# A two-layer hybrid encoder on one Trainium2 core: tile pools opened in another order, so that the matmul operands begin at multiples of 2 KB in each partition

## The chip, the cores and the metric

The kernel runs on one core of one Trainium2 chip. The metric is the device time of one execution in microseconds (us); lower is better. On-chip memory (SBUF) has 128 partitions, and every tile takes the same byte range in each of them. TensorE (PE in the profile) multiplies: a weight load (PEld) puts a stationary block of 128x128 into the array, and a matmul streams a moving block of 128 rows and up to 512 columns past it into PSUM. VectorE (DVE), ScalarE (ACT) and GpSimd (POOL) do elementwise work; SyncE (SP) issues most DMAs.

## The reference, cut to what matters

Two layers; each has a mixing half (windowed attention and an mLSTM side by side) and an MLP half. 256 tokens of width 2048, MLP width 8192, all in float32.

```
def hybrid_layer(x, w_in, ..., w_out, ..., w_up, w_down):
    h = rms_norm(x, g_pre_mix)
    proj = h @ w_in                                   # 2048 x 4624
    ...                                               # attention and mLSTM on slices of proj
    mix = jnp.concatenate([att, mem.astype(att.dtype)], axis=-1) @ w_out
    x = x + rms_norm(mix, g_post_mix)
    h = rms_norm(x, g_pre_mlp)
    u = jnp.square(jax.nn.relu(h @ w_up))             # 2048 x 8192
    x = x + rms_norm(u @ w_down, g_post_mlp)          # 8192 x 2048
    return x
```

## The kernel before, in words

All large products run as three float32r matmuls. Each operand is split into a high part (rounded to float32r) and a low part (what is left), and the product is high*high + high*low + low*high.

**Weights.** They arrive from `wall` in pieces of up to 1 MB, four pieces for one tile of 512 output columns. `load` puts a piece into `raw` by a DMA (SP queue), ACT copies it into `whi` (L186), DVE subtracts and writes `wlo` (L187). `raw` has two buffers (pool `wraw`), `whi` and `wlo` four each (pool `wsp`), so the pieces of the next tile are prepared under the matmuls of this one.

**Tokens.** The normed tokens, the attention output, the mLSTM output and the MLP's hidden values stand transposed, as high and low part, in tiles of 8x2x256 (`hT`, `attT`, `memT`, `h2T`, `uT`; pool `tpool`, 16 KB a buffer, four buffers). One block of 128 features holds 256 high values and behind them 256 low values, 1 KB each.

**Two kinds of matmul.** `mm_k` (L198 to L200) serves the "in", "out" and "down" stages and the first "up" tile: a token block of 128 columns is stationary, and a row of weights (512 columns, 2 KB in each partition; 272 and 256 in two of the "in" tiles) is moving. `mm_stationary` (L267 to L269) serves the other "up" tiles: a weight block of 128 columns is stationary and 256 token columns (1 KB) are moving. Every matmul loads its stationary block anew. The order on each engine is that of the program; waits are semaphores set from the data's dependences.

**Where tiles lie.** A pool takes its place in SBUF when it is opened, and tiles of one buffer follow each other in the order in which they are first asked for. Before the change `const` comes first (with `xs`, the 16 KB of residual stream, at its head), then `tpool`, `apool`, `gpool`, `wraw`, `wsp` and the small ones. 1152 bytes in front of all pools hold the DMA scratch and four constants. So the build gives these starts (bytes in each partition; a 512-wide row of weights that starts at remainder 1728 reaches over the next multiple of 2048, and so does the high half of a token block, which starts at 1664; its low half starts at 640 and does not):

| tile | start before | remainder by 2048 | start after | remainder by 2048 |
|---|---|---|---|---|
| tokens, buffers of `tpool` | 30336 + 16384 i | 1664 | 2048 + 16384 i | 0 |
| `whi` | 134848 + 8192 i | 1728 | 67584 + 8192 i | 0 |
| `wlo` | 167616 + 8192 i | 1728 | 100352 + 8192 i | 0 |
| `raw` | 118464 + 8192 i | 1728 | 133120 + 8192 i | 0 |
| `xs` | 1152 | 1152 | 149504 | 0 |
| `A_mix`, `A_out`, `A_mlp` | 95872 | 1664 | 177824 | 1696 |

In the 272-wide "in" tile the rows of a piece are 1088 bytes apart: before, its four rows start at remainders 1728, 768, 1856 and 896, so the second and fourth row start at a multiple of 128 and do not reach over a multiple of 2048, the first and third start 64 past a multiple of 128 and do. In the 256-wide tile they start at 1728 and 704 in turn, both 64 past a multiple of 128.

Of the kernel before, what the change touches and what calls it, by code (L numbers as in the profile page):

```python
# [10 lines left out]
F32 = mybir.dt.float32  # L11
# [6 lines left out]
P = 128  # L18
SEQ = 256
NT = SEQ // P  # L20
DM = 2048
DFF = 4 * DM
DEPTH = 2
KC = DM // P
# [7 lines left out]
NG = 36  # L32
# [53 lines left out]
@with_exitstack  # L86
def encoder_kernel(ctx, tc, x, wall, rope, conv_w, gate_bias, ml_g, sink, gpre, gpost, out):
    nc = tc.nc
    const = ctx.enter_context(tc.tile_pool(name="const", bufs=1))
    tpool = ctx.enter_context(tc.tile_pool(name="tpool", bufs=4))  # L90
    apool = ctx.enter_context(tc.tile_pool(name="apool", bufs=1))
    gpool = ctx.enter_context(tc.tile_pool(name="gpool", bufs=3))
    wraw = ctx.enter_context(tc.tile_pool(name="wraw", bufs=2))
    wsp = ctx.enter_context(tc.tile_pool(name="wsp", bufs=4))
    f2k = ctx.enter_context(tc.tile_pool(name="f2k", bufs=8))
    f1k = ctx.enter_context(tc.tile_pool(name="f1k", bufs=5))
    small = ctx.enter_context(tc.tile_pool(name="small", bufs=3))
# [2 lines left out]
    psax = ctx.enter_context(tc.tile_pool(name="psax", bufs=4, space=bass.MemoryType.PSUM))  # L100


    xs = const.tile([P, NT, DM], F32, name="xs")

    def load_x(t, n):
        sl = slice(n * 512, (n + 1) * 512)
        nc.sync.dma_start(xs[:, t, sl], x[t * P:(t + 1) * P, sl])

    load_x(0, 0)
    gcol = const.tile([P, 2 * DEPTH, KC], F32, name="gcol")  # L110
    nc.scalar.dma_start(gcol, gpre)
    ident = const.tile([P, P], F32, name="ident")
    make_identity(nc, ident)
# [13 lines left out]
    dmask = const.tile([P, 2, P], F32R, name="dmask")  # L127
    nc.scalar.activation(dmask, mbase, AF.Copy)
    cossin = const.tile([P, 2, NT, HD], F32, name="cossin")
    nhalf = const.tile([P, 4], F32, name="nhalf")  # L130
    nc.gpsimd.memset(nhalf, -0.5)
    gpad = const.tile([P, NT, 2, NG], F32, name="gpad")
    nc.gpsimd.memset(gpad, 0.0)
    ones_r = const.tile([NG, P], F32, name="ones_r")
    nc.gpsimd.memset(ones_r, 1.0)
# [818 lines left out]
```

## Time and profile before

| | |
|---|---|
| median of 3 runs | 2145.48 us (2144.82 to 2150.1) |
| the profiled execution: its own time | 2146.32 us |
| its span, first to last instruction | 2144.5 us |
| PE busy | 2101.9 us, 98% of the span |
| mean granted clock of TensorE | 0.995 |

The span leaves 1.8 us of the execution's time around it. PE is busy from end to end, and the matmuls overlap each other in the record: one shows 0.39 us while the next starts 0.23 us after it. What a matmul costs is therefore read from the distance of starts and not from its duration.

### The profile page before, as it was taken

To read this page: it belongs to the slowest core of one execution; us is meant where nothing else is said; L and a number is where in the kernel's file an instruction comes from. 1 tells how busy PE (TensorE), PEld (TensorE's weight loads), DVE (VectorE), ACT (ScalarE), POOL (GpSimd) and SP (SyncE) were. 2 spreads that over 40 slices of the span, in tenths; PEclk is the share of its full clock that TensorE was granted. 3 is DMA by queue.
4 is the path that set the end of the run, shared out by engine and by line. 5 is a ranking of instruction groups with operands and counts; after the bars stand their busy time and mean duration, and the time that the engine had idled before them with its cause. 6 is when DMAs were issued, how large, how long until landed. Compare 5 with 4: busy or idle time off the path is not lost.

```text
span 2144.5 us, 28977 instructions
## 1 busy us (share of the span) xinstructions
PE 2101.9 (98%) x12412; PEld 1847.2 (86%) x12412; DVE 1134.8 (53%) x1219; ACT 983.1 (46%) x1077; POOL 60.8 (3%) x68
## 2 busy tenths in 40 slices
PE   8999999999999999999999999999999999999998
PEld 6878887988998998898878788879889989989986
DVE  6656566544444444445566656464544454444454
ACT  5445545453443453345354555454444434533542
POOL 0000002000000000000020000030000000000000
PEclk9999999999999999999999999999999999999999
DMA  7434354555555455545444344535555555555553
GB/s 251 165 138 176 119 195 179 197 189 187 194 190 192 175 199 203 187 173 219 169 179 161 134 151 147 206 132 203 206 197 179 195 195 178 197 195 177 197 203 116
DMA packets 62209, 388.37 MB, mean 181 GB/s; under 512 B 9600, under 2 KB 10112, under 8 KB 17280
## 3 DMA queue, kind: packets, MB, share of 16 engines
q1 hardware_dynamic: 61936, 386.48, 51.2%
q8 instruction: 97, 1.59, 0.3%
q14 instruction: 32, 0.26, 0.0%
q10 hardware_dynamic: 144, 0.03, 0.0%
HBM read 384.39 MB, written 2.10 MB: 180 GB/s over the span
## 4 chain that ended last, share of the span: by engine, by line
PE 92%; DVE 2%; ACT 2%; DMA 2%; POOL 1%; issue 1%; SPq 0%; POOLq 0%; DVEq 0%; ACTq 0%
PE mm L200 20%; PE mm L198 19%; PE mm L199 19%; PE mms L267 10%; PE mms L269 10%; PE mms L268 10%; DMA raw<-wall 1%; DVE wlo L187 1%; PE pn L589 1%; PE sc L373 1%; PE po L412 1%; ACT whi L186 1%; DVE xs L787 1%; POOL h2T L320 1%; ACT uz L843 0%
## 5 line engine op out<-in xcount | busy, mean ns | idle before, releaser
L187 DVE TENSOR_TENSOR wlo<-raw,whi 128x2048 fp32r<-128x2048 f32 (+3 forms) x374 | 828.8, 2217 | 885.9 <-ACT whi L186 885.6
L186 ACT ACTIVATE whi<-raw 128x2048 fp32r<-128x2048 f32 (+3 forms) x374 | 693.2, 1854 | 926.9 <-PE mm L200 519.0
L267 PE MATMUL mms<-h2T,whi 128*128 128x256 f32 x1920 | 531.8, 277 | 7.2 <-ACT uz L843 6.6
L268 PE MATMUL mms<-h2T,whi 128*128 128x256 f32 x1920 | 529.9, 276 | 0.0
L269 PE MATMUL mms<-h2T,wlo 128*128 128x256 f32 x1920 | 527.2, 276 | 0.0
L198 PE MATMUL mm<-whi,uT 128*128 128x512 f32 x1024 | 403.7, 394 | 0.0
L200 PE MATMUL mm<-whi,uT 128*128 128x512 f32 x1024 | 401.2, 392 | 0.0
L199 PE MATMUL mm<-wlo,uT 128*128 128x512 f32 x1024 | 397.6, 388 | 0.0
L267 PEld LDWEIGHTS mms<-h2T,whi 128*128 128x128 f32 x1920 | 360.4, 188 | 12.0 <-ACT uz L843 10.6
L268 PEld LDWEIGHTS mms<-h2T,whi 128*128 128x128 f32 x1920 | 360.5, 188 | 0.4
L269 PEld LDWEIGHTS mms<-h2T,wlo 128*128 128x128 f32 x1920 | 358.9, 188 | 0.0
L198 PE MATMUL mm<-whi,hT 128*128 128x512 f32 (+2 forms) x640 | 242.2, 379 | 7.8 <-ACT hT L319 5.8
L200 PE MATMUL mm<-whi,hT 128*128 128x512 f32 (+2 forms) x640 | 242.0, 379 | 0.6 <-POOL hT L320 0.5
L199 PE MATMUL mm<-wlo,hT 128*128 128x512 f32 (+2 forms) x640 | 242.1, 378 | 0.2 <-DVE wlo L187 0.2
L200 PEld LDWEIGHTS mm<-whi,uT 128*128 128x128 f32 x1024 | 192.2, 188 | 44.6
L199 PEld LDWEIGHTS mm<-wlo,uT 128*128 128x128 f32 x1024 | 192.3, 188 | 42.5
L198 PEld LDWEIGHTS mm<-whi,uT 128*128 128x128 f32 x1024 | 192.7, 188 | 37.9
L198 PEld LDWEIGHTS mm<-whi,hT 128*128 128x128 f32 x640 | 121.5, 190 | 29.0 <-ACT hT L319 6.6
L200 PEld LDWEIGHTS mm<-whi,hT 128*128 128x128 f32 x640 | 121.4, 190 | 22.3 <-POOL hT L320 1.4
L199 PEld LDWEIGHTS mm<-wlo,hT 128*128 128x128 f32 x640 | 121.4, 190 | 20.8 <-DVE wlo L187 0.5
L864 DVE SCALAR_TENSOR_TENSOR A_mlp<-mm,s2q,A_mlp 128x512 f32<-128x512 f32 x48 | 34.0, 748 | 38.5 <-PE mm L200 38.5
L198 PE MATMUL mm<-whi,memT 128*128 128x512 f32 x128 | 50.6, 395 | 0.0
(221 smaller groups left out, 1464.4 us busy)
## 6 DMA issues: line engine op xcount, KB each, us to landing
raw<-wall SPq DMA_DIRECT2D x350, 1024.0 KB, 4.8
raw<-wall SPq DMA_DIRECT2D x8, 544.0 KB, 3.6
g<-gpost SPq DMA_DIRECT2D x16, 256.0 KB, 4.4
raw<-wall SPq DMA_DIRECT2D x8, 512.0 KB, 3.4
xs<-x_in SPq DMA_DIRECT2D x8, 256.0 KB, 6.3
raw<-wall SPq DMA_DIRECT2D x8, 256.0 KB, 6.2
y_out<-xs SPq DMA_DIRECT2D x8, 256.0 KB, 2.8
cossin<-rope SPq DMA_DIRECT2D x1, 256.0 KB, 7.2
```

Source lines behind the costliest of these rows:

```text
L186: nc.scalar.activation(hi[:, sl], raw[:, sl], AF.Copy)
L187: nc.vector.tensor_tensor(out=lo[:, sl], in0=raw[:, sl], in1=hi[:, sl].bitcast(F32), op=ALU.subtract)
L198: nc.tensor.matmul(dst, lhsT=xh, rhs=hi, start=(k == 0), stop=False)
L199: nc.tensor.matmul(dst, lhsT=xh, rhs=lo, start=False, stop=False)
L200: nc.tensor.matmul(dst, lhsT=xl, rhs=hi, start=False, stop=(k == KC - 1))
L267: nc.tensor.matmul(ps[:, i], lhsT=hi[:, k], rhs=Tk[:, 0], start=(k == 0), stop=False)
L268: nc.tensor.matmul(ps[:, i], lhsT=hi[:, k], rhs=Tk[:, 1], start=False, stop=False)
L269: nc.tensor.matmul(ps[:, i], lhsT=lo[:, k], rhs=Tk[:, 0], start=False, stop=(k == KC - 1))
L320: (eng or nc.vector).tensor_tensor(out=lo, in0=ps, in1=hi.bitcast(F32), op=ALU.subtract)
L373: nc.tensor.matmul(sc[:, j], lhsT=qT[:, q0 + j, t * P:(t + 1) * P], rhs=kT[:, g], start=(j == 0), stop=False)
L412: nc.tensor.matmul(po[:, j], lhsT=vA[:, kb, g * HD:(g + 1) * HD], rhs=pT[:, kb], start=(kb == 0), stop=(kb == 1))
L864: nc.vector.scalar_tensor_tensor(out=acc[:, t, sl], in0=ps, scalar=s2[t], in1=acc[:, t, sl], op0=ALU.mult, op1=ALU.add)
```

## The change

The pools are opened in another order. A new pool `edge` takes three small tiles that were in `const` (`gcol`, `nhalf`, `gpad`); `nhalf` grows from 4 to 16 columns, and with that `edge` fills exactly the 896 bytes from 1152 to 2048. Behind it stand `tpool`, `wsp` and `wraw`, whose buffers are multiples of 2 KB, and only then `const` and the others. The starts that this gives are in the table above. No buffer is added or dropped. The instructions of every engine stand in the same order with the same waits as before; the one that differs is the fill of `nhalf` (16 columns in place of 4).

```diff
@@ encoder_kernel
     nc = tc.nc
+    edge = ctx.enter_context(tc.tile_pool(name="edge", bufs=1))
+    tpool = ctx.enter_context(tc.tile_pool(name="tpool", bufs=4))
+    wsp = ctx.enter_context(tc.tile_pool(name="wsp", bufs=4))
+    wraw = ctx.enter_context(tc.tile_pool(name="wraw", bufs=2))
     const = ctx.enter_context(tc.tile_pool(name="const", bufs=1))
-    tpool = ctx.enter_context(tc.tile_pool(name="tpool", bufs=4))
     apool = ctx.enter_context(tc.tile_pool(name="apool", bufs=1))
     gpool = ctx.enter_context(tc.tile_pool(name="gpool", bufs=3))
-    wraw = ctx.enter_context(tc.tile_pool(name="wraw", bufs=2))
-    wsp = ctx.enter_context(tc.tile_pool(name="wsp", bufs=4))
...
+    gcol = edge.tile([P, 2 * DEPTH, KC], F32, name="gcol")
+    nhalf = edge.tile([P, 16], F32, name="nhalf")
+    gpad = edge.tile([P, NT, 2, NG], F32, name="gpad")
     xs = const.tile([P, NT, DM], F32, name="xs")
...
-    gcol = const.tile([P, 2 * DEPTH, KC], F32, name="gcol")
...
-    nhalf = const.tile([P, 4], F32, name="nhalf")
     nc.gpsimd.memset(nhalf, -0.5)
-    gpad = const.tile([P, NT, 2, NG], F32, name="gpad")
     nc.gpsimd.memset(gpad, 0.0)
```

## Rows read from the trace of the kernel before

**Rows 1.** The page, part 1: busy time, share of the span, instructions.
```profile
PE 2101.9 (98%) x12412; PEld 1847.2 (86%) x12412; DVE 1134.8 (53%) x1219; ACT 983.1 (46%) x1077; POOL 60.8 (3%) x68
```
**Rows 2.** The page, part 4: the chain that ended last, by engine.
```profile
PE 92%; DVE 2%; ACT 2%; DMA 2%; POOL 1%; issue 1%; SPq 0%; POOLq 0%; DVEq 0%; ACTq 0%
```
**Rows 3.** Groups by shape: busy us, mean ns of one, idle before.
```profile
L187 DVE TENSOR_TENSOR wlo<-raw,whi 128x2048 fp32r<-128x2048 f32 x350 | 803.3, 2296 | 859.7 <-ACT whi L186 859.5
L186 ACT ACTIVATE whi<-raw 128x2048 fp32r<-128x2048 f32 x350 | 671.1, 1917 | 892.6 <-PE mm L200 497.5 <-PE mms L268 207.9 <-DMA raw<-wall 170.1
L267 PE MATMUL mms<-h2T,whi 128*128 128x256 f32 x1920 | 531.8, 277 | 7.2 <-ACT uz L843 6.6 <-ACT whi L186 0.6
L198 PE MATMUL mm<-whi,uT 128*128 128x512 f32 x1024 | 403.7, 394 | 0.0
L198 PE MATMUL mm<-whi,hT 128*128 128x512 f32 x512 | 205.6, 402 | 7.8 <-ACT hT L319 5.8 <-ACT qkn L521 2.0
L198 PE MATMUL mm<-whi,memT 128*128 128x512 f32 x128 | 50.6, 395 | 0.0
L198 PE MATMUL mm<-whi,attT 128*128 128x512 f32 x128 | 50.5, 394 | 0.0
L198 PE MATMUL mm<-whi,h2T 128*128 128x512 f32 x64 | 25.9, 404 | 2.7 <-ACT h2T L319 2.7
```
**Rows 4.** Timeline of PE in a "down" tile: start us, us, what.
```profile
1000.17 0.39 PE L198 MATMUL mm<-whi,uT 128*128 128x512 f32 x1
1000.40 0.39 PE L199 MATMUL mm<-wlo,uT 128*128 128x512 f32 x1
1000.63 0.39 PE L200 MATMUL mm<-whi,uT 128*128 128x512 f32 x1
...
1002.23 0.39 PE L198 MATMUL mm<-whi,uT 128*128 128x512 f32 x1
```
**Rows 5.** Timeline of PE in an "up" tile.
```profile
400.02 0.28 PE L267 MATMUL mms<-h2T,whi 128*128 128x256 f32 x1
400.14 0.28 PE L268 MATMUL mms<-h2T,whi 128*128 128x256 f32 x1
400.25 0.28 PE L269 MATMUL mms<-h2T,wlo 128*128 128x256 f32 x1
400.36 0.28 PE L267 MATMUL mms<-h2T,whi 128*128 128x256 f32 x1
...
401.04 0.28 PE L267 MATMUL mms<-h2T,whi 128*128 128x256 f32 x1
```
**Rows 6.** Windows: length; busy us of PE, PEld, DVE, ACT, POOL; clock; DMA share; GB/s.
```profile
1000.00:1010.00 10.00, 10.00 (x45) 8.21 (x44) 7.20 (x6) 4.18 (x7) 0.00 (x0) 1.00 0.54 193
1315.00:1317.00 2.00, 2.00 (x19) 2.00 (x19) 2.00 (x7) 2.00 (x8) 0.00 (x0) 1.00 0.41 94
1325.60:1328.20 2.60, 2.60 (x26) 2.60 (x25) 1.24 (x6) 2.59 (x5) 0.00 (x0) 1.00 0.99 296
```
**Rows 7.** Timeline of PE in the 256-wide "in" tile of layer 2, two stretches.
```profile
1315.29 0.28 PE L198 MATMUL mm<-whi,hT 128*128 128x256 f32 x1
...
1316.70 0.28 PE L198 MATMUL mm<-whi,hT 128*128 128x256 f32 x1
...
1325.68 0.28 PE L198 MATMUL mm<-whi,hT 128*128 128x256 f32 x1
...
1328.06 0.28 PE L198 MATMUL mm<-whi,hT 128*128 128x256 f32 x1
```
**Rows 8.** Timeline of PE in the 272-wide "in" tile of layer 1.
```profile
99.88 0.28 PE L198 MATMUL mm<-whi,hT 128*128 128x272 f32 x1
...
100.63 0.29 PE L198 MATMUL mm<-whi,hT 128*128 128x272 f32 x1
...
101.38 0.28 PE L198 MATMUL mm<-whi,hT 128*128 128x272 f32 x1
...
102.12 0.28 PE L198 MATMUL mm<-whi,hT 128*128 128x272 f32 x1
...
102.88 0.39 PE L198 MATMUL mm<-whi,hT 128*128 128x512 f32 x1
```
**Rows 9.** The chain in the first 60 us: start us, us, what.
```profile
3.54 7.00 DMA xs<-x_in
...
24.63 8.55 DMA raw<-wall
```
**Rows 10.** Timeline of POOL at the start.
```profile
1.47 0.10 POOL L131 MEMSET nhalf<- 128x4 f32 x1
1.50 0.22 POOL L133 MEMSET gpad<- 128x144 f32 x1
```
**Rows 11.** Spans and mean granted clock.
```profile
core 0: 2144.5 us, clock 0.995
```

## The prediction

> **What bounds the kernel now.** I read the busy shares first, then the chain of work that ended last, then the groups by shape, and last the timeline of PE, row by row, in the places that the change could touch. PE is busy 98% of the span [rows 1] and makes up 92% of the chain; DVE, ACT and DMA have 2% each [rows 2]. The splitting of the weights, the largest work outside PE, waits and is not waited for: ACT stands idle before L186 because PE still holds the buffers, and DVE stands idle before L187 because ACT has not finished [rows 3]. So the time is the number of matmuls by the distance of their starts, and an edit that only moves tiles counts if it changes that distance.
>
> The distance has two values. In a "down" tile nine 512-wide matmuls lie between 1000.17 and 1002.23 us [rows 4]: 2.06/9 = 0.2289 us each. In an "up" tile nine 256-wide ones lie between 400.02 and 401.04 [rows 5]: 0.1133 us. The clock granted in the first place is 1.00, the level of 2.4 GHz [rows 6], where one column a cycle would be 0.2133 and 0.1067. So 15.6 ns of each 512-wide matmul and 6.7 ns of each 256-wide one are something else, and the question of this change is whether they hang on the operands' addresses. Counts: with three lines each, the 512-wide matmuls are 3 x (1024 + 512 + 128 + 128 + 64) = 5568, the 256-wide "up" ones 3 x 1920 = 5760 [rows 3]. That is 5568 x 0.2289 + 5760 x 0.1133 = 1274.5 + 652.6 = 1927 us of the span.
>
> **The change part by part.** Its parts are four: where the moving and stationary operands start, where the elementwise engines read and write, where DMAs land, and a wider fill.
>
> *Matmul operands.* Three rows speak on it. First, in the "up" tiles the high half of the tokens (moving in L267 and L269) reaches over a multiple of 2048 bytes and the low half (L268) does not. Start to start, L267 takes 0.12 us, L268 and L269 0.11 each [rows 5], which is 0.1133 in steps of 10 ns; reaching over costs nothing that shows. The weakness is that a weight load runs beside each of these and may set the pace. Second, in the 256-wide "in" tile weights are moving, at the same two starts all through the tile. Between 1315.29 and 1316.70 us twelve matmuls take 0.1175 us each; between 1325.68 and 1328.06 twenty-one take 0.1133 [rows 7], at a clock of 1.00 in both [rows 6]. The same instructions at the same starts run at two paces, so at least this 4.2 ns does not come from where a row begins. Third, in the 272-wide tile two of the four rows of a piece reach over a multiple of 2048 and two do not. Six matmuls on one row take 0.75, 0.75, 0.74 and 0.76 us in turn [rows 8]: the rows that reach over take 0.745 on the mean, the others 0.755. If anything, not reaching over is dearer, by 0.01/6 = 1.7 ns a matmul. From these rows I take 0 for the operands. The bounds: minus 4.2 ns (from the slow pace of [rows 7] to the fast one) for each of the 5568 matmuls with weights moving, 23 us gained, or 47 us if it grows with the width; plus 1.7 ns for each of 5568 + 5760, 19 us lost. Zero is the nearest to the first row, which has the shift itself in it and shows none.
>
> One page of the Trainium skill speaks of a matmul's price without a word on addresses: "TensorE: Matmul & The Clock Gate" (Wait — 56ns, not 53.3ns?) gives N/2.4 GHz plus 2.5 ns for back-to-back matmuls, 215.8 ns at 512 columns. The rows have 228.9, so here the measurement differs from the page; if all of that difference went, an estimate by that page, the kernel would gain 5568 x 13.1 = 73 us.
>
> *Elementwise engines.* `raw`, `whi` and `wlo` have one remainder among themselves before and after (1728, then 0), so their relation is not altered. DVE takes 2296 ns and ACT 1917 ns for 2048 columns [rows 3]; whichever way these went by some per cent, PE covers it: ACT is idle 892.6 us before these instructions. If that cover were gone each per cent would cost 7 to 8 us. I take 0.
>
> *DMAs.* `raw` and `xs` land at other remainders. Transfers stand in the chain with 2% [rows 2], and the two long pieces are at the start: 7.00 us for `xs` and 8.55 us for `raw` [rows 9]. No row tells what a start at a multiple of 2048 gives. A tenth of both, either way, is 1.6 us; I take 0 and keep 1.6 for the range. The page "DMA: Bandwidth & Descriptors" (How a descriptor splits into AXI transactions) says that a transaction must start at a multiple of 256 bytes; a row of `xs` (2048 bytes from remainder 128 by 256) would then need nine in place of eight and a row of `raw` 33 in place of 32, an estimate from that page of 0.8 + 0.3 = 1.1 us gained. No run here shows it yet.
>
> *The fill of `nhalf`.* 16 columns in place of 4. The fill of 4 columns takes 0.10 us and that of 144 takes 0.22 [rows 10], so the growth is under 0.12 us, on POOL before the first matmul; it counts as 0.
>
> The sum is 0. The profiled execution's own time is 2146.32 us with a span of 2144.5, 0.8 us over the median of 2145.48; I forecast the median, 2145 us. What differs between runs without a change of code is of the size of the range of the three runs, 5.3 us; part of it can be stretches at the lower clock, since the mean clock is 0.995 and not 1 [rows 11]. About 0.3%, 6.4 us, is what a measurement of this kernel can tell from no change.
>
> **The rivals.**
>
> *Faster: the new starts bring the faster pace to the matmuls with weights moving.* The place is every "in", "out" and "down" tile. For it: there is an excess of 15.6 ns on 512 columns that no wait explains, it is the same with other engines' load, and two paces exist [rows 7]. Against it: both paces occur at one and the same start. The price is 23 us by a fixed 4.2 ns (2122 us) and 47 us if it doubles with the width (2098). It decides if the distance in the "down" tiles falls from 0.2289 to 0.2247 or less. By the page on TensorE it could come to 2072; that sentence carries no chance of its own beyond this rival's.
>
> *Slower: operands that all start at multiples of 128 disturb each other.* PE streams a moving row while it loads the next stationary block. Before, tokens start at a multiple of 128 and weights 64 past one; only the second and fourth rows of the 272-wide pieces have both at a multiple, and these are the dearer ones [rows 8]. After, all 512-wide and all "up" matmuls are in that case. For it: the 1.7 ns. Against it: the rows are read in steps of 10 ns and hold one piece. The price is 1.7 x 11328 = 19 us, 2164 us; scaled with the width (512/272 and 256/272) it is 17.8 + 9.2 = 27 us, 2172. It decides from 0.6 ns a matmul, where 11328 of them exceed 6.4 us.
>
> That the change does not do what it says is excluded: the starts of the built kernel are the ones in the table.
>
> **How the numbers follow.** No change has 0.70: two rows speak for it and one weakly against. Faster has 0.16, slower 0.14. Half of the faster cases lie near 2122 and half lower; of the slower ones about half lie up to 2166. A range from 2118 to 2166 holds 0.70 + 0.07 + 0.07 = 0.84, and cut closer it would lose the near end of both rivals. The likeliest case's own range is 2139 to 2152. Faster by over 0.3% is 0.16, within it 0.70, slower 0.14.
>
> **What would show it.** If the forecast is right, the distances of starts stay 0.229 us in the "down" tiles and 0.113 in the "up" tiles, DVE stays at 2296 ns and ACT at 1917 for 2048 columns, and PE busy stays at 2102 us. Wrong would be another distance in a "down" tile (the faster rival, or the slower) or in an "up" tile (the slower one alone). A shift of the time with unchanged distances would point to the DMAs of the start or to clock stretches; the first 50 us and the mean clock would show these.

## The result: slower by 1.2%

The changed kernel has a median of 2171.84 us (2169.64 to 2173.81), the kernel before 2146.63 us (2144.82 to 2150.1), four runs each on the same chip. The ratio is 1.0116, with a 95% interval from 1.0101 to 1.0130. The forecast was no change, 2145 us in a range up to 2166; the time lies above the range.

The profiled execution of the changed kernel took 2173.81 us with a span of 2172.0, 27.5 us more than before, at the same mean clock of 0.995 [rows 11]. Two lines were added above the code, so L198 to L200 are now L200 to L202, and L267 to L269 are L269 to L271. The page's busy times, and the shares of the chain of waits by engine:

```profile
PE 2130.1 (98%) x12412; PEld 1884.1 (87%) x12412; DVE 1136.4 (52%) x1219; ACT 983.3 (45%) x1077; POOL 60.7 (3%) x68
```
```profile
PE 93%; DVE 2%; ACT 2%; DMA 1%; POOL 1%; issue 1%; SPq 0%; POOLq 0%; DVEq 0%; ACTq 0%
```

PE is busy 28.2 us longer than in [rows 1] with the same 12412 matmuls, the weight loads, which overlap them, 36.9 us longer, and the other engines are within 2 us of what they were. So the time went into the matmuls themselves. The groups by shape say into which (busy us, mean ns of one, idle before and what ended it):

```profile
L189 DVE TENSOR_TENSOR wlo<-raw,whi 128x2048 fp32r<-128x2048 f32 x350 | 803.2, 2295 | 881.4 <-ACT whi L188 881.1
L188 ACT ACTIVATE whi<-raw 128x2048 fp32r<-128x2048 f32 x350 | 670.6, 1916 | 909.0 <-PE mm L202 493.4 <-PE mms L270 317.9 <-DMA raw<-wall 89.1
L269 PE MATMUL mms<-h2T,whi 128*128 128x256 f32 x1920 | 544.4, 284 | 7.3 <-ACT uz L845 7.3
...
L200 PE MATMUL mm<-whi,uT 128*128 128x512 f32 x1024 | 398.4, 389 | 0.0
```

Against [rows 3] the two splitting instructions are the same to 1 ns, PE waits no longer before L269 (7.3 us, 7.2 before), and the matmuls moved in **opposite directions**: the 256-wide "up" ones show 284 ns in place of 277, the 512-wide "down" ones 389 in place of 394. The timeline of PE gives the distances of starts, first in a "down" tile, then in an "up" tile (start us, us, what):

```profile
999.68 0.39 PE L200 MATMUL mm<-whi,uT 128*128 128x512 f32 x1
999.91 0.39 PE L201 MATMUL mm<-wlo,uT 128*128 128x512 f32 x1
1000.14 0.39 PE L202 MATMUL mm<-whi,uT 128*128 128x512 f32 x1
...
1002.40 0.39 PE L200 MATMUL mm<-whi,uT 128*128 128x512 f32 x1
```
```profile
400.15 0.28 PE L269 MATMUL mms<-h2T,whi 128*128 128x256 f32 x1
400.27 0.28 PE L270 MATMUL mms<-h2T,whi 128*128 128x256 f32 x1
400.39 0.28 PE L271 MATMUL mms<-h2T,wlo 128*128 128x256 f32 x1
400.51 0.28 PE L269 MATMUL mms<-h2T,whi 128*128 128x256 f32 x1
...
401.23 0.28 PE L269 MATMUL mms<-h2T,whi 128*128 128x256 f32 x1
```

Twelve "down" matmuls take 2.72 us, 0.2267 each, against 0.2289 in [rows 4]. Nine "up" matmuls take 1.08 us, 0.1200 each, against 0.1133 in [rows 5]. Over the whole trace, wherever four matmuls of one kind follow each other (without the few that a wait or a stretch at the lower clock made over 5% longer), the mean distances are 113.42 ns before and 119.97 after in the "up" tiles, 228.97 and 227.01 for the 512-wide matmuls. The sum is 5760 x 6.55 = +37.7 us and 5568 x -1.96 = -10.9 us, together +26.8 of the 27.5. What is left to explain is why.

### The profile page after: what moved, and what is told of

Its sections match the earlier page's. It is cut to its first block, busy times and chain, and to the rows that moved or that the text cites. A ratio compares the mean times of both kernels' runs of the same rounds, so it can differ in the third digit from the quotient of the medians.

```text
span 2172.0 us, 28977 instructions
## 1 busy us (share of the span) xinstructions
PE 2130.1 (98%) x12412; PEld 1884.1 (87%) x12412; DVE 1136.4 (52%) x1219; ACT 983.3 (45%) x1077; POOL 60.7 (3%) x68
## 4 chain that ended last, share of the span: by engine, by line
PE 93%; DVE 2%; ACT 2%; DMA 1%; POOL 1%; issue 1%; SPq 0%; POOLq 0%; DVEq 0%; ACTq 0%
PE mm L202 19%; PE mm L201 19%; PE mm L200 19%; PE mms L269 11%; PE mms L271 11%; PE mms L270 11%; DMA raw<-wall 1%; PE pn L591 1%; PE sc L375 1%; DVE xs L789 1%; PE po L414 1%; DVE wlo L189 1%; POOL h2T L322 0%; ACT uz L845 0%; ACT whi L188 0%
## 5 line engine op out<-in xcount | busy, mean ns | idle before, releaser
L269 PE MATMUL mms<-h2T,whi 128*128 128x256 f32 x1920 | 544.4, 284 | 7.3 <-ACT uz L845 7.3
L270 PE MATMUL mms<-h2T,whi 128*128 128x256 f32 x1920 | 542.6, 283 | 0.0
L271 PE MATMUL mms<-h2T,wlo 128*128 128x256 f32 x1920 | 539.8, 283 | 0.0
L200 PE MATMUL mm<-whi,uT 128*128 128x512 f32 x1024 | 398.4, 389 | 0.0
L202 PE MATMUL mm<-whi,uT 128*128 128x512 f32 x1024 | 398.1, 389 | 0.0
L269 PEld LDWEIGHTS mms<-h2T,whi 128*128 128x128 f32 x1920 | 368.4, 192 | 11.9 <-ACT uz L845 11.5
L270 PEld LDWEIGHTS mms<-h2T,whi 128*128 128x128 f32 x1920 | 368.4, 192 | 0.3
L271 PEld LDWEIGHTS mms<-h2T,wlo 128*128 128x128 f32 x1920 | 366.9, 192 | 0.0
L200 PE MATMUL mm<-whi,hT 128*128 128x512 f32 (+2 forms) x640 | 242.6, 380 | 8.7 <-ACT hT L321 6.5
L202 PE MATMUL mm<-whi,hT 128*128 128x512 f32 (+2 forms) x640 | 242.0, 379 | 0.3 <-POOL hT L322 0.2
L200 PEld LDWEIGHTS mm<-whi,uT 128*128 128x128 f32 x1024 | 192.2, 188 | 39.5
L202 PEld LDWEIGHTS mm<-whi,uT 128*128 128x128 f32 x1024 | 192.2, 188 | 39.4
L200 PEld LDWEIGHTS mm<-whi,hT 128*128 128x128 f32 x640 | 121.9, 190 | 29.1 <-ACT hT L321 7.4
L202 PEld LDWEIGHTS mm<-whi,hT 128*128 128x128 f32 x640 | 121.7, 190 | 21.9 <-POOL hT L322 1.2
L200 PE MATMUL mm<-whi,memT 128*128 128x512 f32 x128 | 50.4, 394 | 0.0
```

Source lines behind the costliest of these rows:

```text
L200: nc.tensor.matmul(dst, lhsT=xh, rhs=hi, start=(k == 0), stop=False)
L202: nc.tensor.matmul(dst, lhsT=xl, rhs=hi, start=False, stop=(k == KC - 1))
L269: nc.tensor.matmul(ps[:, i], lhsT=hi[:, k], rhs=Tk[:, 0], start=(k == 0), stop=False)
L270: nc.tensor.matmul(ps[:, i], lhsT=hi[:, k], rhs=Tk[:, 1], start=False, stop=False)
L271: nc.tensor.matmul(ps[:, i], lhsT=lo[:, k], rhs=Tk[:, 0], start=False, stop=(k == KC - 1))
```

## The experiments

Two theories. The **own-start theory**: a matmul's price hangs on where one operand begins (tokens or weights, for themselves), at a multiple of 128 or 2048 bytes or not. The **distance theory**: PE streams one row while it loads the next stationary block, and the price hangs on how far these two starts lie apart, by remainder. Before, weights minus tokens is 64 by 256 in every full-width matmul (1728 - 1664 = 64, and the 1 KB to the low part changes nothing); after, it is 0. A third possibility is that only the order of the regions or their place in SBUF counts. Below, "distance d" is the start of the weights minus that of the tokens, in bytes, by remainder of 256.

**One gap.** A small pool between `tpool` and `wsp` leaves the tokens where the change put them and moves the weights on; 64 bytes here, and other sizes in the runs below:

```diff
     tpool = ctx.enter_context(tc.tile_pool(name="tpool", bufs=4))
+    gpool0 = ctx.enter_context(tc.tile_pool(name="gap", bufs=1))
     wsp = ctx.enter_context(tc.tile_pool(name="wsp", bufs=4))
...
+    gap = gpool0.tile([P, 16], F32, name="gap")
+    nc.gpsimd.memset(gap, 0.0)
```

> The changed kernel with 64 bytes put between the tokens and the weights: tokens stay at multiples of 2 KB, high and low parts of the weights (and raw) begin 64 past one, as far from the tokens by remainder of 256 as in the kernel before. Theory 1 (what counts is how far the start of the streamed row lies from that of the stationary block that is loaded beside it, by its remainder of 256): both distances are those of the kernel before, 0.1133 us in the up tiles and 0.2289 in the down tiles, time 2146 us (2140 to 2152). Theory 2 (what counts is the start of the streamed row by itself, a multiple of 2 KB being dear for the tokens and cheap for the weights): the up tiles keep 0.120, the down tiles go back to 0.2289, time 2172 + 5568 x 2.2 ns = 2184 us. Theory 3 (the order in which the regions lie, or that pools lie lower): nothing changes against the changed kernel, 2172 us.

Measured: 2145.91 us, ratio to before 0.9994 (0.9980 to 1.0007). The loss is gone with 64 bytes, with the tokens still at a multiple of 2 KB and the regions in the order of the changed kernel, so that order is not what costs. Its "down" tile and its "up" tiles, from the timeline of PE:

```profile
999.67 0.39 PE L203 MATMUL mm<-whi,uT 128*128 128x512 f32 x1
...
1002.42 0.39 PE L203 MATMUL mm<-whi,uT 128*128 128x512 f32 x1
```
```profile
400.62 0.28 PE L272 MATMUL mms<-h2T,whi 128*128 128x256 f32 x1
...
401.64 0.28 PE L272 MATMUL mms<-h2T,whi 128*128 128x256 f32 x1
...
572.05 0.28 PE L272 MATMUL mms<-h2T,whi 128*128 128x256 f32 x1
...
573.82 0.28 PE L272 MATMUL mms<-h2T,whi 128*128 128x256 f32 x1
```

The twelve 512-wide ones are back at 0.2292. The "up" tiles have two paces now: nine in 1.02 us at 400 us, 0.1133, and fifteen in 1.77 us at 572 us, 0.1180. We come back to that. This profiled execution is the longest of the ten: 2154.94 us at a mean clock of 0.996, where three others at 0.996 took 2145.5 to 2145.9. The 9 us fit its slow stretches (5760 x 1.8 ns = 10 us), so the others probably had fewer of them; no trace of theirs shows it.

**Both starts moved.** `nhalf` is widened, so that tokens and weights both begin 64 past a multiple of 2 KB, at distance 0:

```diff
-    nhalf = edge.tile([P, 16], F32, name="nhalf")
+    nhalf = edge.tile([P, 32], F32, name="nhalf")
```

> The changed kernel with everything from the tokens on moved by 64 bytes: neither tokens nor weights begin at a multiple of 128, but they keep their distance from each other (0 by remainder of 256). Theory 1 (distance of the two starts): 0.120 us in the up tiles, 0.2267 in the down tiles as in the changed kernel, 2172 us (2166 to 2178). Theory 2 (the start of the streamed row by itself): the down tiles go back to 0.2289 us and the up tiles to something else than 0.120, 0.1133 if the multiple of 128 was what made them dear: 2146 us.

Measured: 2173.35 us, ratio 1.0115 (1.0098 to 1.0131), as the changed kernel. The timeline, "up" and "down":

```profile
400.07 0.28 PE L269 MATMUL mms<-h2T,whi 128*128 128x256 f32 x1
...
401.87 0.28 PE L269 MATMUL mms<-h2T,whi 128*128 128x256 f32 x1
```
```profile
999.70 0.39 PE L200 MATMUL mm<-whi,uT 128*128 128x512 f32 x1
...
1002.42 0.39 PE L200 MATMUL mm<-whi,uT 128*128 128x512 f32 x1
```

Fifteen in 1.80 us are 0.1200, twelve in 2.72 are 0.2267. Neither operand begins at a multiple of 128 here, and the paces are those of distance 0. The own-start theory falls. The rows of weights reach over a multiple of 2048 again here, and W, the distance of the 512-wide matmuls over the whole trace, is the same to 0.01 ns, so reaching over costs nothing.

**Other distances.** The same gap with other sizes:

> The changed kernel with 128 bytes between the tokens and the weights. No run has this distance except some rows of the 272-wide tile (0.755 us for six matmuls, as dear as at distance 0). Theory 1: new distances of starts in both kinds of tiles, other than 0.1133/0.2289 and 0.120/0.2267 in at least one of them; by the 272-wide rows nearer to the changed kernel, 2160 to 2180 us. Theory 2: up tiles 0.120, down tiles 0.2289, 2184 us.

> The changed kernel with 192 bytes between the tokens and the weights. Seen from the weights this is the distance that the tokens had to the weights in the kernel before, so by theory 1 the down tiles stand to the tokens as the up tiles stood to the weights before (256 columns at 0.1133 us, so at 512 columns 0.2200 to 0.2267), and the up tiles as the down tiles stood before (slow pace of the 256-wide tile, 0.1178): 2172 - 5760 x 2.2 ns - 5568 x (0 to 6.7) ns = 2122 to 2159 us. Theory 2: up tiles 0.120, down tiles 0.2289, 2184 us.

> The changed kernel with 256 bytes between the tokens and the weights. If the distance counts by its remainder of 256, this is distance 0 again: 0.120 us in the up tiles, 0.2267 in the down tiles, 2172 us (2166 to 2178). If it counts by its remainder of 512 (the length of a stationary block) or of 2048 (a row), another pair than that, as each other distance tried so far gave another pair.

> The changed kernel with 32 bytes between the tokens and the weights. If two streams collide only while they are in the same 64 bytes of 256, half a step gives distances of starts between those at 0 and at 64: 0.1133 to 0.120 in the up tiles, 0.2267 to 0.229 in the down tiles, 2146 to 2172 us. If a finer alignment counts (starts at multiples of 64), both kinds of tiles are dearer than at 0 and at 64: over 2185 us.

> The changed kernel with 96 bytes between the tokens and the weights; with w160 and w224 it completes the steps of 32 bytes by remainder of 256. So far the down tiles (512 columns) have 0.2267 us at distance 0, 0.2333 at 32, 0.2290 at 64, 0.2317 at 128, 0.2333 at 192, and the up tiles (256 columns; their distance runs the other way) 0.1200, 0.1183, 0.1133 or 0.1178, 0.1180, 0.1177. Theory 1 (distance of the two streams): a pair of its own. Odd steps of 32 (one of the two starts is no multiple of 64) were dear for the down tiles at 32; if that is the rule, 0.2333 here too, and 2185 to 2195 us.

> 160 bytes between tokens and weights. Theory 1: a pair of its own; if odd steps of 32 are dear as a rule, 0.2333 us in the down tiles and 2185 to 2195 us; if distance 0 is the only good place of the down tiles because both streams enter the same 64 bytes together, anything from 0.229 to 0.2333.

> 224 bytes between tokens and weights, which is 32 before a multiple of 256. Theory 1: a pair of its own; if the two streams only count by how far apart they are, whichever is ahead, 0.2333 us in the down tiles and 0.1183 in the up tiles as at 32, 2190 us; if the order counts, another pair.

Measured, with the runs above and below for comparison (T: mean distance of starts of the "up" matmuls, W: of the 512-wide ones, both in ns; paces: the distances that whole stretches of "up" matmuls hold, a stretch being what runs between two waits or other instructions of PE; sum: 2146.3 + 5.760 x (T - 113.42) + 5.568 x (W - 228.97), to be held against the time of the same profiled execution):

| kernel | d | T | paces of the "up" stretches | W | sum, us | profiled execution, us | median, us | ratio (95%) |
|---|---|---|---|---|---|---|---|---|
| before | 64 | 113.42 | 113.4; 117.8 in one short stretch | 228.97 |  | 2146.3 | 2146.63 |  |
| after | 0 | 119.97 | 120.0 | 227.01 | 2173 | 2173.8 | 2171.84 | 1.0116 |
| gap 256 | 0 | 119.97 | 120.0 | 227.03 | 2173 | 2172.5 | one run |  |
| both moved 64 | 0 | 119.97 | 120.0 | 227.02 | 2173 | 2176.3 | 2173.35 | 1.0115 (1.0098 to 1.0131) |
| gap 32 | 32 | 118.33 | 118.3 | 233.32 | 2199 | 2190.8 | one run |  |
| gap 64 | 64 | 115.22 | 113.4 and 117.8 | 229.00 | 2157 | 2154.9 | 2145.91 | 0.9994 (0.9980 to 1.0007) |
| gap 96 | 96 | 118.16 | 117.3, 118.7 and 120.0 | 233.35 | 2198 | 2194.2 | one run |  |
| gap 128 | 128 | 118.68 | 118.7; 119.9 in two short ones | 232.49 | 2196 | 2190.6 | 2190.6 | 1.0193 (1.0178 to 1.0208) |
| gap 160 | 160 | 119.98 | 120.0 | 234.24 | 2213 | 2206.4 | one run |  |
| gap 192 | 192 | 117.17 | 117.8; 113.3 in six of 26 | 233.32 | 2192 | 2187.8 | 2185.11 | 1.0167 (1.0150 to 1.0184) |
| gap 224 | 224 | 117.03 | 116.7 and 117.8 | 233.28 | 2191 | 2186.3 | one run |  |

The sums meet the executions within about 8 us; most of those that miss by more than 4 ran at a mean clock of 0.997 or 0.998 in place of 0.995, and 0.003 of 2146 us is 6 us. Three things follow. The price follows the distance: equal distances with different starts (before and gap 64; after, gap 256 and both moved) give equal paces for the 512-wide matmuls, and at distance 0 also for the "up" ones. It does not simply fall with more room between the starts: 32 is as bad as 192. And a start at a multiple of 128 is not what costs: at 128 every start is one, at 192 only the tokens' is, and both are slow. The two kinds have different best distances: 0 for W, where no other distance reaches 227.0, and 64 for T. But T is a mean over paces, and the 113.3 of distance 64 turns up at 192 too, in fewer stretches (fifteen matmuls in 1.70 us at 1489 us, in 1.77 at 572):

```profile
1489.09 0.28 PE L272 MATMUL mms<-h2T,whi 128*128 128x256 f32 x1
...
1490.79 0.28 PE L272 MATMUL mms<-h2T,whi 128*128 128x256 f32 x1
...
572.27 0.28 PE L272 MATMUL mms<-h2T,whi 128*128 128x256 f32 x1
...
574.03 0.28 PE L272 MATMUL mms<-h2T,whi 128*128 128x256 f32 x1
```

Four forecasts were missed: 128 (2160 to 2180 us), 192 (2122 to 2159) and 160 (2185 to 2195) came out dearer, and 32 did not lie between 0 and 64 for the 512-wide matmuls. So the theory says that the distance counts; it did not foretell what each distance costs.

**The same distance with the roles exchanged.** The 256-wide "in" tiles have the weights moving and the tokens stationary, the "up" tiles the other way round, at the same width. Counted as start of the streamed operand minus start of the stationary one, d is the distance of the first, and 256 - d that of the second. Mean distances of starts in ns, with the gap of the run:

| streamed minus stationary | "in", weights streamed | "up", tokens streamed |
|---|---|---|
| 0 | 119.7 (after) | 120.0 (after) |
| 32 | 116.9 (gap 32) | 117.0 (gap 224) |
| 64 | 117.8 (gap 64) | 117.2 (gap 192) |
| 96 | 119.8 (gap 96) | 120.0 (gap 160) |
| 128 | 118.9 (gap 128) | 118.7 (gap 128) |
| 160 | 118.1 (gap 160) | 118.2 (gap 96) |
| 192 | 116.0 (gap 192) | 115.2 (gap 64) |
| 224 | 118.3 (gap 224) | 118.3 (gap 32) |

They agree within 0.3 ns, but for 64 and 192, which have the two paces of 113.3 and 117.8 in varying shares. So at one width the price goes with this distance, its direction included, and not with which of the two tensors is streamed. Fifteen matmuls of an "in" tile (gap 32) and of an "up" tile (gap 224) take 1.75 us each:

```profile
1341.19 0.28 PE L203 MATMUL mm<-whi,hT 128*128 128x256 f32 x1
...
1342.94 0.28 PE L203 MATMUL mm<-whi,hT 128*128 128x256 f32 x1
```
```profile
551.21 0.28 PE L272 MATMUL mms<-h2T,whi 128*128 128x256 f32 x1
...
552.96 0.28 PE L272 MATMUL mms<-h2T,whi 128*128 128x256 f32 x1
```

**Each kind at its best distance.** The stationary `uT`, `hT`, `attT` and `memT` stay at distance 0; the `h2T` of the "up" tiles begins 192 bytes into a buffer that is 256 larger, so its distance is 64:

```diff
+SHIFT = 48
+PAD = 64
...
+    def one_T(name):
+        o = SHIFT if name[:3] == "h2T" else 0
+        flat = tpool.tile([P, 4096 + PAD], F32R, tag="T", name=name)
+        return flat[:, o:o + 4096].rearrange("p (k j s) -> p k j s", k=8, j=2)
```

> The changed kernel with the tokens that are streamed in the up tiles (h2T) begun 192 bytes into their buffers (the buffers grow by 256), so that they lie to the weights as in the kernel before, while the other tokens stay at distance 0 from the weights. Theory 1 (only the distance of the two streams counts, and each kind of tile can have its own): up tiles 0.1133 us as before, down tiles 0.2267 as after; 2147 - 5568 x 2.2 ns = 2135 us (2128 to 2142), faster than both. Theory 2 (the start by itself): the down tiles keep 0.2267 or go to 0.229, the up tiles are at a start that is no multiple of 128: no forecast below 2146.

Measured: 2146.9 us, ratio 1.0002 (0.9991 to 1.0013), not the 2128 to 2142 that were expected. W is 227.03 as hoped, a gain of 10.8 us, but T is 115.51 and not 113.42, which gives 12.0 us back. The timeline shows the two paces in two "up" stretches of one execution:

```profile
572.01 0.28 PE L271 MATMUL mms<-h2T,whi 128*128 128x256 f32 x1
...
573.71 0.28 PE L271 MATMUL mms<-h2T,whi 128*128 128x256 f32 x1
...
714.06 0.28 PE L271 MATMUL mms<-h2T,whi 128*128 128x256 f32 x1
...
715.83 0.28 PE L271 MATMUL mms<-h2T,whi 128*128 128x256 f32 x1
```

Fifteen in 1.70 us, 0.1133, then fifteen in 1.77, 0.1180. No stretch changes its pace on the way; it can change where PE waits or does something else. The long stretches (382 or 384 matmuls) that follow a wait for ACT are at 0.1134 in seven of eight, the stretches of 290 that begin straight behind a "down" tile at 0.1178 in all six. The short ones of 96 follow a wait for ACT as well and are slow in seven of eight, so the wait by itself does not choose. In the profiled execution with the 64-byte gap it is the other way round: six of the eight long stretches are slow, those of 290 and of 96 fast. In the execution of before that was profiled all but one stretch of 49 are fast.

**What chooses the pace?** One or two small transpositions on PE ahead of the first "up" tile of a block, to let the stretch of 290 begin differently:

```diff
     def mm_stationary(key, T, after):
...
+        if key[3] == 0:
+            nudge = psax.tile([P, 4, P], F32, tag="ax", name="nudge")
+            for i in range(1):
+                nc.tensor.transpose(nudge[:, i], ident, ident)
```

> h2off with one small transposition on PE (128 columns, nothing reads it) ahead of the first up tile of the second, third and fourth MLP block. In h2off the stretch of 290 matmuls that begins there without a wait ran at 0.1178 us in all six places, while the 381 that follow a wait of PE ran at 0.1134 in seven of eight. If the pace is set by how the stretch is entered (theory 1 with a start in time: load and stream settle into one of two patterns and keep it until PE waits again), the 290 change to 0.1134: 6 x 290 x 4.4 ns = 7.7 us less than h2off's profiled run, about 2136 us, faster than both kernels by 0.5%. If the pace comes from something else at that place, it stays 0.1178 and the time 2144 to 2149.

> As h2nudge1 with two transpositions, an entry at another moment: by theory 1 either of the two paces can come out in the 290, and in the 381 after the next wait; about 2136 or 2144 us. If the place and not the entry decides: 0.1178 in the 290 as in h2off.

Measured: 2147.07 us, ratio 0.9999 (0.9987 to 1.0012), and 2146.51, ratio 0.9993 (0.9982 to 1.0003). The stretches of 290 stay at 0.1178 and the long ones at 0.1134; T is 115.31 in both. How the stretch is entered, as far as a transposition alters it, does not choose.

Then two distances beside 64 for the "up" tiles, with 0 kept for the others (`SHIFT` 44 and 52), in search of one with a single fast pace:

> h2off with the streamed tokens of the up tiles 176 bytes into their buffers in place of 192, 16 bytes nearer; the down tiles stay at distance 0 (0.2267 us). By theory 1 the up tiles get a pace of this distance; 64 gives 0.1133 or 0.1178 and the steps beside it (32 and 96) 0.1170 and 0.1180, so 80 should lie between. If the two paces of 64 come from sitting at an edge, one side of it has 0.1133 alone: 2134 us; else 0.1178 or more, 2153 us and up.

> h2off with the streamed tokens 208 bytes into their buffers, 16 bytes further; distance 48 in the up tiles, 0 in the down tiles. As for h2off176: 0.1133 us alone and 2134 us if 64 sits at the edge of a good stretch on this side, else 0.1178 or more and 2153 us and up.

Measured: at distance 80, T is 119.26 and the time 2172.32, ratio 1.0117 (1.0100 to 1.0134). At distance 48, T is 118.95 and the time 2167.37, ratio 1.0096 (1.0081 to 1.0112). The good distance is narrow: 16 bytes to either side cost 5.5 ns or more on the mean against the fast pace.

**Who is the partner of the streamed row?** Two runs change only what the weight load reads. In the first, on top of the 128-byte gap, each stationary token block but those of `h2T` holds high and low values in turn, so that the load steps 8 bytes from column to column:

```diff
+        return flat[:, :4096].rearrange("p (k s j) -> p k j s", k=8, j=2)
```

> Distance 128 as in w128, but the tokens that are stationary (hT, uT, attT, memT) hold high and low values in turn, so that a weight load of 128 columns steps over 8 bytes a column and covers 1024 bytes in the time in which it covered 512: it then moves through memory as fast as the streamed row beside it. The arithmetic is the same. Theory 1 in its stricter form (a load at half the speed of the stream is overtaken by it and the stream stops at each meeting; 16 cycles of 2.4 GHz, 6.7 ns, each): streams of one speed 128 bytes apart do not meet, the down tiles fall from 0.232 to 0.2133 to 0.2200 us, time 2190.6 - 5568 x (12 to 18.7 ns) = 2087 to 2124 us. Rival (the excess belongs to the change of the stationary block, whatever is read): 2190 us. Rival (a load with steps is slower by itself): weight loads longer than 188 ns and 2190 us or more.

Measured: 2190.73 us, ratio 1.0199 (1.0174 to 1.0224), W 231.46 against 232.49 with the plain gap of 128; the 256-wide "in" matmuls went the other way, from 118.9 to 121.0. The load itself takes longer, 196 ns in place of 188 with the plain gap:

```profile
L205 PEld LDWEIGHTS mm<-whi,uT 128*128 128x128 f32 x1024 | 200.3, 196 | 36.3
```

In its strict form the theory had the row overtake a load of half its speed and stop at each meeting; with steps of 8 bytes the two were to advance at equal speed and not to meet, and the time was to fall to 2087 to 2124 us. It did not, so this form falls, or its premise on the speeds does: no run shows how fast a load advances. In the second run the load of every stationary token block reads one column 128 times, with the starts of the changed kernel (the kernel no longer computes the layer then):

```diff
-        xh, xl = (Tk[:, j, t * P:(t + 1) * P] for j in range(2))
+        xh, xl = (Tk[:, j, t * P:t * P + 1].to_broadcast([P, P]) for j in range(2))
```

> The changed kernel; in the in, out and down tiles every weight load reads one token column 128 times instead of 128 columns (what is computed there is wrong; number, order and width of all matmuls stay, and the streamed rows are the same bytes). Theory 1 (the excess of a matmul is the weight load's reading of memory getting in the way of the stream's): the down tiles leave 0.2267 us, since the load now stays in 4 bytes of memory and meets the stream elsewhere or less; towards 0.2133 to 0.2200 if staying put is cheap. Rival (the excess is the change of stationary blocks, or the stream alone): 0.2267 us stays. The up tiles keep 0.120 in either case.

Measured: 2190.82 us in one run; the "up" tiles, whose loads are untouched, stay at 119.95. The load and the matmul of a "down" tile by group, and the timeline of the tile:

```profile
L200 PEld LDWEIGHTS mm<-whi,uT 128*128 128x128 f32 x1024 | 193.6, 189 | 43.4
L200 PE MATMUL mm<-whi,uT 128*128 128x512 f32 x1024 | 403.6, 394 | 0.0
```
```profile
1004.04 0.40 PE L200 MATMUL mm<-whi,uT 128*128 128x512 f32 x1
...
1009.60 0.40 PE L200 MATMUL mm<-whi,uT 128*128 128x512 f32 x1
```

24 matmuls take 5.56 us, 0.2317 each, against 0.2267 after the change. The streamed rows, their starts and the load's length (189 ns, 188 before the edit) are the same; only the bytes that the load reads, and its step from column to column, are others. So what the load reads does set the pace of the matmuls beside it, and it is the partner. A load that stays on one spot was to be the cheaper one. At 512 columns it is dearer, but in the 256-wide "in" tiles it is cheaper: 113.3 ns in four of five stretches, where the changed kernel has 120.0. Fifteen matmuls take 1.80 us in the changed kernel and 1.70 in this run:

```profile
1330.09 0.28 PE L200 MATMUL mm<-whi,hT 128*128 128x256 f32 x1
...
1331.89 0.28 PE L200 MATMUL mm<-whi,hT 128*128 128x256 f32 x1
```
```profile
1339.20 0.28 PE L200 MATMUL mm<-whi,hT 128*128 128x256 f32 x1
...
1340.90 0.28 PE L200 MATMUL mm<-whi,hT 128*128 128x256 f32 x1
```

The Trainium skill says on "TensorE: Matmul & The Clock Gate" (Step-by-step: what each phase is for) that PE has two independent read ports and that loading the next tile's weights doesn't take read bandwidth from the running matmul. As far as the time goes, this run and the table differ from that sentence: 5 ns on 227 by the load's bytes alone, and up to 7 ns by distance. The measurement decides here; whether it is read bandwidth that is lost, no run shows.

## Why the prediction was wrong, point by point

**What bounds the kernel** was right: time is the number of matmuls by the distance of their starts. The counts, multiplied by the measured distances, give 26.8 of the 27.5 us.

**The failed step is the 0 for the matmul operands**, and within it the question. The first row, [rows 5], was asked whether reaching over a multiple of 2048 costs anything; it rightly showed no, but that is a statement about one operand's own start. In [rows 4] and [rows 5] alike the weights stand 64 bytes from the tokens, so these rows could not speak of any other distance. "It has the shift itself in it" was wrong: the shift that mattered, of one operand against the other, was in neither. In place of the 0 the runs show +6.55 ns for each of 5760 "up" matmuls and -1.96 for each of 5568 of 512 columns, +26.8 us.

**The bound of 1.7 ns** was the term that was mis-sized. It came from the 272-wide tile [rows 8], where the four rows of a piece stand at distances 64, 128, 192 and 0 in turn. This was the one place before in which the distance varied, and it was read by remainders of each start. The same tile in the changed kernel, where the rows stand at 0, 64, 128 and 192:

```profile
98.36 0.28 PE L200 MATMUL mm<-whi,hT 128*128 128x272 f32 x1
...
99.11 0.28 PE L200 MATMUL mm<-whi,hT 128*128 128x272 f32 x1
...
99.86 0.29 PE L200 MATMUL mm<-whi,hT 128*128 128x272 f32 x1
...
100.62 0.28 PE L200 MATMUL mm<-whi,hT 128*128 128x272 f32 x1
```

Six matmuls take 0.75 or 0.76 us at 0, 64 and 128, as before. At 272 columns the distance hardly matters (by 2 ns a matmul), at 256 it is worth 6.6 and at 512 up to 7. To carry the 1.7 ns to the other widths, by count or scaled, was the error. A slip beside it: by its own halves of 0.16 and 0.14 the range holds 0.85, not 0.84.

**The two paces of [rows 7]** were taken as a price that new starts might remove. They are two paces of one distance, 64, and the runs with 64 or 192 in the "up" tiles have them too (0.1134 and 0.1178). The changed kernel has one pace in the 256-wide "in" tile, 0.1200, above both.

**The slower rival** named the right engine and two operands that disturb each other. Its scaled price of 2172 is the measured time, but by accident: it had 17.8 + 9.2 us on both kinds, and the runs show 37.7 - 10.9. Its mechanism, starts at a multiple of 128, fell with the both-moved run, where no operand has one and the loss is the same. The **faster rival** was right on the 512-wide matmuls alone: a gain of 2 ns each, less than half of the 4.2 it needed.

**The terms taken at nothing held.** DVE has 2295 ns and ACT 1916 against 2296 and 1917. The fill of `nhalf` takes 0.11 us against 0.10 [rows 10]:

```profile
1.47 0.11 POOL L134 MEMSET nhalf<- 128x16 f32 x1
```

The DMAs of the start are worth about 1 us here, within the 1.6 that the range kept for them: PE is that much further after 50 us. In the windows of the changed kernel (length; busy us of PE, PEld, DVE, ACT, POOL; clock; DMA share; GB/s) PE has 50 and 135 instructions, 50 and 130 before, and 11.46 + 29.91 us busy against 12.06 + 28.76; five matmuls are 1.1 us:

```profile
0.00:19.10 19.10, 11.46 (x50) 8.91 (x51) 10.77 (x23) 13.75 (x30) 3.92 (x20) 1.00 0.88 291
19.10:50.00 30.90, 29.91 (x135) 23.92 (x134) 22.58 (x35) 16.30 (x19) 0.55 (x1) 1.00 0.76 236
```

The second long piece of the chain, `raw`, takes 7.43 us where it took 8.55 [rows 9], as much less. Whether that comes from its start is not settled: over all runs the same piece takes 7.43 to 8.76 us where it begins at a multiple of 256 (8 runs, mean 8.0) and 7.28 to 9.06 where it doesn't (10 runs, mean 8.5). The gain that the prediction had estimated from the Trainium skill's page "DMA: Bandwidth & Descriptors" (How a descriptor splits into AXI transactions), 0.3 us for this piece, is smaller than this scatter. The long piece of `xs` takes 7.03 us against 7.00, without the 0.8 of the estimate. A smaller effect goes with the start on the last of the eight transfers of `xs`: 6.91 to 6.98 us from issue to landing in seven of the eight runs where `xs`, and `raw` with it, begins at a multiple of 256 (7.62 in the eighth), and 7.19 to 7.74 in the ten others. Some 0.25 of 7.2 us is 3%, where an estimate by that page, one transaction of nine, would be 11%; the page's words are on what a transaction reads, and what moved here is where it writes.

**What stays open**: by what the distance works, since room between the starts doesn't explain the order in the table, and a change of what the load reads moved the two widths in opposite directions; and what chooses among the paces of one distance. Because of the second, no version here is faster than the kernel before: with every "up" stretch at the fast pace, an estimate from these rows, the version with both best distances would come to about 2146.3 - 10.9 = 2135 us, which was not reached.

## What to carry to other kernels

On back-to-back float32r matmuls that each load a new stationary block, treat the distance between the streamed row's start and the stationary block's, by remainder of 256 bytes, as a knob: 64 bytes of padding moved this kernel by 1.2%, and the worst of the distances tried costs 2.6% (2206.4 us against 2150.06 for the kernel before beside it, one run each). A layout is not better for round starts, and one width's answer doesn't carry to another. Before you call a layout neutral, ask for which pairs of operands the trace has more than one distance; where all rows have the same one, it says nothing of others.

## What had not been expected of the hardware

The pace of a stretch of equal matmuls moves by a few ns with the operands' distance: 113.4 to 120.0 ns for 256 columns, 227.0 to 234.2 ns for 512. At 256 columns one distance can have two or three paces (113.4 and 117.8 at 64 and at 192; 117.3, 118.7 and 120.0 at 96), and a stretch holds one of them until PE waits or does something else. None of this seems to hang on the load of the other engines: in the changed kernel four "up" matmuls in a row lie 120.0 ns apart both where DVE, ACT and POOL are idle throughout and where DVE and ACT are busy throughout, and the 512-wide ones 226.9 and 226.7. The length of the weight load doesn't tell the pace either: in the "up" tiles it is 192 ns in the changed kernel and 188 with the gap of 160, and T is 120.0 in both (first the changed kernel, then that run; both are groups of the weight loads):

```profile
L269 PEld LDWEIGHTS mms<-h2T,whi 128*128 128x128 f32 x1920 | 368.4, 192 | 11.9 <-ACT uz L845 11.5
```
```profile
L272 PEld LDWEIGHTS mms<-h2T,whi 128*128 128x128 f32 x1920 | 361.5, 188 | 12.0 <-ACT uz L848 11.5 <-ACT whi L191 0.2
```
